# Sixteen products that nobody reads, between the last up products of each layer and the loop for further experts

## The chip, the core and the metric

The kernel runs on one core of one Trainium2 chip. The metric is the device time of one execution in microseconds (us). The engines are named as in the profile: PE is TensorE (PEld its weight loads), DVE is VectorE, ACT is ScalarE, POOL is GpSimd, and SP is SyncE, whose queue issues most of the transfers (DMAs). A name with a q (PEldq, SPq) is the sequencer of that engine, which takes its instructions in the order of the program.

## The reference

Two layers of a block with four mixers and a mixture of experts, on 256 tokens and 256 context tokens of width 1024. What matters here is the end of each layer: the experts, their sum, and what the next layer starts with.

```python
def moe(h, w_router, b_router, w1, w3, w2):
    ...
    gate = jnp.sum(jax.nn.one_hot(top_i, N_EXPERTS, dtype=F32) * top_w[..., None], axis=-2)
    out = 0.0
    for e in range(N_EXPERTS):
        he = jax.nn.silu(h @ w1[e]) * (h @ w3[e])
        out = out + gate[..., e:e + 1].astype(h.dtype) * (he @ w2[e])
    return out

def reference(...):
    for l in range(DEPTH):
        ...
        x = x + gt2 * moe(h2, router_w, router_b, moe_w1[l], moe_w3[l], moe_w2[l])
        ...
    return rms_norm(x, final_norm_g)
```

Each token goes to 2 of 16 experts. `h @ w1` and `h @ w3` are the up products, `he @ w2` the down products.

## The kernel before, in words

Each layer `l` runs through `mix` (input projection, the four mixers), `wout` and the router, and then `moe`. The tokens of an expert are gathered into a slot of fixed size (`SLOT`); the 16 slots run one after the other, as generators that `moe` advances in turn, so that the products of one expert lie between those of its neighbours. The weights of an expert are six blocks of 1 MB: 0 to 3 for the up products, 4 and 5 for the down products. SP fetches them ahead into rings of buffers (`fetch`, `pump`); the ring `raw` has three buffers, which experts, the input projection of the next layer (`in_win_dram`) and its modulation vectors (`in_wada_dram`) share.

The last expert of a layer, slot 15, has 64 rows (`expert32`). Its up products go to `sc`, two at a time in the two halves of the array: 32 products with 512 columns each. Then ACT copies `sc` to `al`, PE transposes `al` (`tp<-cst,al`), ACT and DVE make `silu(..) * ..` of it, and the 16 down products follow (`mm<-raw,ah`).

Between the up products and these transposes stands `extras(l)`: a loop over further slots of 128 rows, for experts with more tokens than their slot. How often it runs (`nx`, tile `rnx`) is known on the chip only; with these inputs it is 0 times in both layers, so that its body never runs. Every engine loads `rnx` into a register (line 2069), compares and branches (line 2070), and on the way past the loop all engines join: SP waits until each of its transfers has landed, each engine waits until its own work before the loop is done, and each reads the counts of all others before it goes on. These are the `EVENT_SEMAPHORE` instructions of line 2070.

Behind the loop come the down products, `combine_rows` (SP loads the sums of the other experts from the buffer `ybd` in HBM), and `combine`: for each piece of 128 rows by 512 columns PE adds the row of `ybd` (times the identity, `cst`) and the scattered result of the last expert in PSUM, and DVE, with POOL, adds it to the residual `yf`. Layer 0 has eight such pieces, layer 1 four. `self.gate_open += 1; self.pump()` lets SP go on to the weights of the next layer. After `combine` of layer 0 stands `ln1` of layer 1 with the input projection; after that of layer 1 `final`, the last norm and the store.

The order of the instructions within an engine is made by a scheduler from the priorities of the program; `tc.issue_after(x)` puts what stands under it directly behind instruction `x`. A helper records every operation, so that nearly all rows of the profile carry line 396.

Of the kernel before, what the change touches and what calls it, by code (L numbers as in the profile page):

```python
# [12 lines left out]
BF16 = mybir.dt.bfloat16  # L13
# [25 lines left out]
)  # L39
NRAW = 3  # L40
PARTED = (0, 4)
STAT = 2
RESERVE = (8, 8)
ADA_SLACK = (-1.0, 1.0)
# [16 lines left out]
TILE = [np.cumsum([0] + [-(-n // P) for n in SLOT[l]]).tolist() for l in range(L)]  # L61
ENDS = (STAT, NE - 1)

# [97 lines left out]
def _constants():  # L161
# [23 lines left out]
    for l in range(L):  # L185
        order = np.argsort([-n for n in SLOT[l][STAT:]], kind="stable")
        rk = np.full(16, -1)
        rk[STAT + order] = np.arange(NE - STAT)
        put(("rk", l), rk[None, :])
# [213 lines left out]
class Kern:  # L403
# [167 lines left out]
    def fetch(self, src):  # L571
        l = self.l
        n2, n3, n4 = BUFS[f"R{l}"]["raw2"], BUFS[self.scope]["raw3"], PARTED[l]
        r = self.wi % (n2 + NRAW + n3 + n4)
# [479 lines left out]
    def put(self, *ts):  # L1054
        for t in ts:
            (self.lent if id(t) in self.lentids else self.own).append(t)
# [671 lines left out]
    def route(self, l, NT):  # L1728
# [66 lines left out]

        nd = NE - STAT
        key, cap = f([P, 16], "key"), f([P, 16], "cap")
# [5 lines left out]
        along = lambda t: t[:, None, :].to_broadcast([P, nd, nd])  # L1803
        tt(big, along(key[:, STAT:]), down(key[:, STAT:]), op=ALU.is_gt)
        nc.vector.reduce_sum(rk, big, axis=AX.X)
        tt(sel, along(rk), down(self.C(("rk", l))[:, STAT:]), op=ALU.is_equal)
        nc.vector.memset(cap[:, 0:STAT], float(SLOT[l][0]))
# [141 lines left out]
    def moe(self, l, route):  # L1949
        nc, tc = self.nc, self.tc  # L1950
        self.yi, self.gi, self.wi = 0, 0, len(self.pre)
        xg, sl = {}, {}
        both = lambda e: [e] + ["x"] * (l == 0 and e == TWO)
        gens, srcs = {}, {}

        def source(e):
            if e not in srcs:
                srcs[e] = (self.wdyn(l, self.rt["idx"][0:1, e - STAT:e - STAT + 1]) if e >= STAT
                           else lambda c: self.I["wmoe"][self.wpos(l, e, c)])
            return srcs[e]  # L1960

        def begin(e):
            if self.whole(l, e):
                t = TILE[l][e]
                half = (self.row2[:, t:t + 1], self.slot_of(self.rt["tab2"][:, t])[1]) if SLOT[l][e] == HALF else None
                gens[e] = self.expert32(l, source(e), (xg.pop(e), *sl[e]), SLOT[l][e], half, last=e == NE - 1)
            else:
                gens[e] = self.expert(l, source(e), [(xg.pop(n), *sl[n]) for n in both(e)], min(P, SLOT[l][e]), ahead=NPRE * (e == 0))
            next(gens[e])

        first, i = self.first_slots(l)
        xg.update(enumerate(first))
        with tc.issue_after(i.ins):
            for _ in range(3):
                next(route)
        for e in range(NE):
            for n, t in zip(both(e), range(TILE[l][e], TILE[l][e + 1])):
                sl[n] = self.slot_of(self.rt["tab"][:, t])
        self.row2 = self.sx([P, TILE[l][NE]], "rrow2", I32)
        begin(0)  # L1980
        next(gens[0])
        for e in range(NE):
            if e == NE - 1:
                self.combine_g2(l)
                while self.wi < len(USE[l]):
                    self.pre.append(self.fetch(source(USE[l][self.wi][0])(USE[l][self.wi][1])))
            if STAT <= e + 2 < NE:
                for n in both(e + 2):
                    xg[n] = self.gather(l, *sl[n], m=min(P, SLOT[l][e + 2]))
            if e == 0:  # L1990
                nc.gpsimd.tensor_scalar(self.row2, self.rt["tab2"][:, :, 0], 2.0, self.half, op0=ALU.mult, op1=ALU.add)

            with tc.issue_after(self.rt["slots"].ins) if e == 0 else ExitStack():
                for j in range(2):
                    if e or j:
                        next(gens[e])
                    if e:
                        next(gens[e - 1], None)
                next(gens[e])
            if e:  # L2000
                next(gens[e - 1], None)
            if e + 1 in ENDS:
                for _ in gens[e]:
                    pass
                begin(e + 1)
                continue
            if e + 1 < NE:
                begin(e + 1)
            next(gens[e])


        self.extras(l)
        for _ in gens[NE - 1]:
            pass
        with tc.issue_after(self.last_y.ins):
            self.combine_rows(l)
        self.gate_open += 1
        self.pump()
        with tc.issue_after(self.last_y.ins), tc.issue_after(self.last_mm.ins):
            self.combine(l)  # L2020
# [399 lines left out]
```

## Time and profile before

| | |
|---|---|
| median of 3 runs | 1255.08 us (1253.22 to 1255.55) |
| the profiled execution | 1252.16 us, of which its span, first to last instruction, is 1250.5 us |
| busy: PE, DVE, ACT, POOL | 89%, 54%, 40%, 14% of the span |
| mean granted clock of PE | 0.946 of full speed |
| DMA, mean over the span | 267 GB/s |
| layer 0: last up product ends, transposes behind the loop start | 688.2 us, 695.0 us |
| layer 1: the same | 1221.2 us, 1224.8 us |

Times in the rows are microseconds from the start of the span. The granted clock 1.00 is 2.4 GHz, 0.50 is 1.2 GHz; a row of a stretch in which it changed shows a value between.

### The profile page before, as it was taken

Reading aid. Unit: us, or ns where it says so; the run is one execution under the profiler, and the core shown is the slowest. Engines: PE = TensorE matmul, PEld = TensorE weight load, DVE = VectorE, ACT = ScalarE, POOL = GpSimd, SP = SyncE. Lnnn points to the kernel's source line nnn. Section 1 sums busy time; section 2 is a strip of 40 time slices with the busy share of each in tenths; the row PEclk is TensorE's granted clock in tenths of the full one; section 3 lists DMA queues with packets and bytes.
Section 4 is the critical chain, followed back from the end, with each engine's and each line's share of the span. In section 5 each row is a group of like instructions: output and inputs, shape, how many; then the busy total and the mean of one; then the engine's idle time right before and its main releaser. Section 6 shows DMA issues by size and latency. Waiting matters only on the chain. (4 is left out here: it accounts for less than half of the span.)

```text
span 1250.5 us, 16252 instructions
## 1 busy us (share of the span) xinstructions
PE 1107.6 (89%) x5537; PEld 684.9 (55%) x5537; DVE 679.4 (54%) x1761; ACT 496.8 (40%) x818; POOL 169.5 (14%) x210
## 2 busy tenths in 40 slices
PE   4999999997995999999888779999986599999974
PEld 2677677765884766555444257776675233333321
DVE  6496579788668863554434548779897200000003
ACT  5231652667324853554434333283662121111112
POOL 0100200100003420211100000010010321111102
PEclk9999999998896999999989889999888699999997
DMA  8673654352936998999993735355358999999992
GB/s 307 246 275 110 221 214 160 136 181 93 366 139 228 353 353 309 359 373 378 383 381 124 299 147 198 101 205 192 129 180 341 381 373 390 371 398 387 397 408 101
DMA packets 66809, 334.08 MB, mean 267 GB/s; under 512 B 13389, under 2 KB 14893, under 8 KB 34977
## 3 DMA queue, kind: packets, MB, share of 16 engines
q1 hardware_dynamic: 54864, 312.39, 65.7%
q0 software_dynamic: 11424, 19.54, 6.0%
q8 instruction: 46, 0.75, 0.2%
q10 hardware_dynamic: 432, 1.05, 0.2%
q14 instruction: 43, 0.34, 0.1%
HBM read 317.54 MB, written 19.15 MB: 269 GB/s over the span
## 5 line engine op out<-in xcount | busy, mean ns | idle before, releaser
L396 DVE TENSOR_TENSOR lo<-raw,hi 128x1024 fp32r<-128x1024 f32 x172 | 206.1, 1221 | 122.0 <-ACT hi L396 120.8
L396 PE MATMUL sc<-raw,ah 128*64 128x512 f32 (+3 forms) x750 | 212.4, 602 | 6.4 <-DMA raw<-in_wmoe_dram 4.4
L396 ACT CAST hi<-raw 128x1024 fp32r<-128x1024 f32 x169 | 171.7, 1048 | 101.8 <-PE mm L396 53.4
L396 DVE TENSOR_TENSOR ah<-al,tp 128x256 f32<-128x256 f32 x21 | 8.8, 420 | 232.9 <-ACT al L396 232.9
L396 PEld LDWEIGHTS sc<-raw,ah 128*64 128x64 f32 (+3 forms) x750 | 62.9, 142 | 117.3 <-issue 100.2
L396 PE MATMUL mm<-hi,ah 128*128 128x512 f32 (+3 forms) x264 | 109.1, 417 | 6.0 <-ACT hi L396 5.6
L396 PE MATMUL mm<-raw,ah 128*64 128x512 f32 (+3 forms) x378 | 110.2, 620 | 3.5 <-DVE rel L396 1.9
L396 PE MATMUL mm<-lo,ah 128*128 128x512 f32 (+3 forms) x264 | 107.6, 407 | 1.6 <-DVE lo L396 1.5
L396 PE MATMUL mm<-hi,al 128*128 128x512 f32 (+3 forms) x264 | 106.9, 407 | 0.3 <-DVE al L396 0.3
L396 PE MATMUL mm<-ah,hi 128*128 128x512 f32 (+1 forms) x224 | 87.0, 393 | 0.8 <-DVE ah L396 0.8
L396 PE MATMUL mm<-ah,lo 128*128 128x512 f32 (+1 forms) x224 | 83.8, 375 | 0.9 <-DVE lo L396 0.9
L396 PE MATMUL mm<-al,hi 128*128 128x512 f32 (+1 forms) x224 | 83.7, 374 | 0.0
L396 PE MATMUL sc<-hi,ah 128*128 128x512 f32 (+3 forms) x176 | 73.6, 419 | 3.7 <-ACT hi L396 3.7
L396 PE MATMUL sc<-lo,ah 128*128 128x512 f32 (+3 forms) x176 | 72.2, 410 | 3.1 <-DVE lo L396 2.9
L396 PE MATMUL sc<-hi,al 128*128 128x512 f32 (+3 forms) x176 | 71.9, 408 | 1.8 <-DVE al L396 1.8
L396 PE MATMUL ad<-raw,cT 128*32 128x256 f32 (+1 forms) x512 | 68.2, 519 | 4.9 <-DMA raw<-in_wada_dram 3.4
L396 PEld LDWEIGHTS mm<-raw,ah 128*64 128x64 f32 (+3 forms) x378 | 33.9, 147 | 65.3 <-issue 55.3
L396 PEld LDWEIGHTS mm<-hi,ah 128*128 128x128 f32 (+3 forms) x264 | 49.7, 189 | 28.9 <-issue 7.8
L396 PEld LDWEIGHTS mm<-lo,ah 128*128 128x128 f32 (+3 forms) x264 | 50.0, 189 | 16.0 <-DVE lo L396 4.9
L396 PEld LDWEIGHTS mm<-hi,al 128*128 128x128 f32 (+3 forms) x264 | 49.9, 189 | 11.7 <-DVE al L396 1.0
L396 PEld LDWEIGHTS mm<-ah,hi 128*128 128x128 f32 x224 | 42.2, 191 | 23.0 <-issue 12.2
L396 POOL DMA_INDIRECT xg<-h2d,rtab x29 | 32.8, 1131 | 123.3 <-PE tp L396 115.1
(434 smaller groups left out, 1817.7 us busy)
## 6 DMA issues: line engine op xcount, KB each, us to landing
raw<-in_wmoe_dram SPq DMA_DIRECT2D x168, 1024.0 KB
raw<-in_wada_dram SPq DMA_DIRECT2D x32, 1024.0 KB
raw<-in_win_dram SPq DMA_DIRECT2D x24, 1024.0 KB
raw<-in_wmoe_dram SPq DMA_DIRECT2D x48, 512.0 KB
raw<-in_wad_dram SPq DMA_DIRECT2D x16, 1024.0 KB
raw<-in_wout_dram SPq DMA_DIRECT2D x8, 1024.0 KB
x<-in_tok_dram SPq DMA_DIRECT2D x8, 512.0 KB
raw<-ybd SPq DMA_DIRECT2D x6, 512.0 KB
```

The source lines that it names most:

```text
L396: r = f(*a, **k)
```

## The change

A new table `WARM` gives a count for each layer, and `moe` issues that many products directly behind the last up product of slot 15, ahead of `extras`: the constant `ones_b` (128 by 128, bf16, all ones) with the first 512 bf16 columns of the table of constants `cst`. All write the same PSUM buffer of the pool `mm`, each from the start, and nothing reads it.

```diff
+WARM = (16, 16)
...
+        ps = self.psmm()
+        with tc.issue_after(self.last_mm.ins):
+            for _ in range(WARM[l]):
+                nc.tensor.matmul(ps, lhsT=self.ones_b, rhs=self.cst.bitcast(BF16)[:, 0:512], start=True, stop=True)
         self.extras(l)
         for _ in gens[NE - 1]:
             pass
```

On PE, at the loop of layer 1, the last up products (`sc<-raw,ah`) stand before directly ahead of the load of `rnx`; the wait for PE_49, PE's own count, is the one for its work before the loop.

```order
L396 MATMUL sc_10216<-raw_10200,ah_10190 64x512
L396 MATMUL sc_10216<-raw_10204,ah_10190 64x512
L2069 TENSOR_LOAD rnx_8954 [waits DVE_49]
L2070 COMPARE_AND_BRANCH
L2070 UNCONDITIONAL_BRANCH [waits PE_49]
```

Now, in the same place, with 16 weight loads and 16 products:

```order
L397 MATMUL sc_10233<-raw_10217,ah_10207 64x512
L397 MATMUL sc_10233<-raw_10221,ah_10207 64x512
L397 LDWEIGHTS ones_b
L397 MATMUL mm_10251<-cst,ones_b 128x512 [waits PE_49]
L397 LDWEIGHTS ones_b
L397 MATMUL mm_10251<-cst,ones_b 128x512
...
L2074 TENSOR_LOAD rnx_8971 [waits DVE_49]
L2075 COMPARE_AND_BRANCH
L2075 UNCONDITIONAL_BRANCH [waits PE_49]
```

The new products stand between the last up products and the join, whose wait for PE's count now takes them in. The same 32 instructions stand ahead of the loop of layer 0.

On SP, ahead of the loop of layer 0, the last block of the last expert (`raw_6052`) is followed by the join, which waits for all transfers. Before:

```order
L396 DMA raw_6050<-in_wmoe_dram 128x2048 [waits DMAHW1_49,PE_49]
L396 ISA
L396 DMA raw_6052<-in_wmoe_dram 128x2048 [waits DMAHW2_49,DVE_49]
L2069 TENSOR_LOAD rnx_3739 [waits DVE_49]
L2070 COMPARE_AND_BRANCH
L2070 UNCONDITIONAL_BRANCH [waits SP_sequencer_49,DMAHW0_49,DMAHW1_49,DMAHW2_49,DMAHW3_49,DMAHW4_49,DMAHW5_49,DMAHW6_49,DMAHW7_49]
```

Now:

```order
L397 DMA raw_6052<-in_wmoe_dram 128x2048 [waits DMAHW2_49,DVE_49]
L2074 TENSOR_LOAD rnx_3739 [waits DVE_49]
L2074 ISA x2
L397 DMA raw_6359<-in_win_dram 128x2048 [waits DMAHW6_49,DVE_49]
L2075 COMPARE_AND_BRANCH
L2075 UNCONDITIONAL_BRANCH [waits SP_sequencer_49,DMAHW0_49,DMAHW1_49,DMAHW2_49,DMAHW3_49,DMAHW4_49,DMAHW5_49,DMAHW6_49,DMAHW7_49]
```

The first block of the next layer's input projection (1 MB) has moved from behind the loop to ahead of it.

On SP, directly behind the loop of layer 0, before:

```order
L2069 ISA x2
L396 DMA raw_6342<-in_win_dram 128x2048
L396 DMA raw_6344<-in_win_dram 128x2048
L396 DMA raw_6336<-ybd_222 128x1024 x2
L396 DMA raw_6339<-ybd_222 128x1024 x2
L396 DMA raw_6346<-in_wada_dram 128x2048 [waits PE_49]
```

Now:

```order
L397 DMA raw_6361<-in_win_dram 128x2048
L397 DMA raw_6363<-in_wada_dram 128x2048 [waits PE_49]
L397 DMA raw_6353<-ybd_222 128x1024 x2
L397 DMA raw_6356<-ybd_222 128x1024 x2
L397 DMA raw_6483<-in_wada_dram 128x2048 [waits DVE_49]
```

The first block of `in_wada_dram`, which waits for PE, has moved ahead of the four loads of `ybd`. With it one product of that block (`ad<-raw,cT`) has moved ahead of `combine` on PE, and the first two splits of the first `in_win_dram` block (`hi<-raw` on ACT, `lo<-raw,hi` on DVE) have moved ahead of the last expert's scaling. In layer 1 no instruction but the new ones has moved, and the rest of the program stands as before.

## Rows read from the trace of the kernel before

**Rows 1.** The page, its first line.

```profile
span 1250.5 us, 16252 instructions
```

**Rows 2.** Chain of work that ended last: start us, us, what.

```profile
1226.84 5.82 PE mm L396 x16
```

**Rows 3.** Timeline, end of layer 1: start us, us, engine, what, xcount [idle before <-releaser].

```profile
1217.59 3.65 PE L396 MATMUL sc<-raw,ah 128*64 128x512 f32 x14 [0.76 <-SPq L2070]
...
1224.78 1.12 PE L396 MATMUL tp<-cst,al 128*128 128x128 f32 x4 [3.55 <-SPq L2070]
1225.90 0.81 SPq L396 DMA_DIRECT2D raw<-ybd  x2
...
1229.71 4.67 POOL L396 TENSOR_TENSOR raw<-raw,raw 128x1024 f32<-128x1024 f32 x2 [17.33 <-DMA raw<-ybd]
```

**Rows 4.** Line 2070, layer 1, by stretches: xcount, ns min/median/max, first to last start us.

```profile
L2070 PEldq EVENT_SEMAPHORE  x13: 51/51/51, 1221.3 to 1224.4; - x13
...
L2070 PEldq EVENT_SEMAPHORE  x3: 51/51/51, 1221.8 to 1222.0; - x3
...
L2070 SPq EVENT_SEMAPHORE  x3: 17/17/17, 1224.0 to 1224.1; - x3
...
L2070 SPq EVENT_SEMAPHORE  x11: 27/28/28, 1224.8 to 1225.4; - x11
```

**Rows 5.** Stretches, layer 1: us, busy PE PEld DVE ACT POOL, PE clock, DMA share, GB/s.

```profile
1224.70:1226.00 1.30, 1.12 (x4) 0.72 (x4) 0.00 (x0) 0.07 (x1) 0.00 (x0) 0.50 0.01 6
...
1231.00:1232.00 1.00, 1.00 (x6) 0.31 (x4) 0.00 (x0) 0.00 (x0) 1.00 (x1) 0.90 0.00 0
```

**Rows 6.** Timeline of PE at full clock: single products, four transposes, 16 paired products.

```profile
663.33 0.39 PE L396 MATMUL sc<-hi,al 128*80 128x512 f32 x1
...
668.37 0.40 PE L396 MATMUL sc<-hi,ah 128*80 128x512 f32 x1
...
1149.47 0.66 PE L396 MATMUL tp<-cst,al 128*128 128x128 f32 x4 [0.68 <-ACT al L396]
...
1154.18 3.60 PE L396 MATMUL mm<-raw,ah 128*64 128x512 f32 x16
```

**Rows 7.** Timeline of PE, then a stretch as in rows 5.

```profile
672.20 0.49 PE L396 MATMUL tp<-cst,s 80*128 80x80 f32 x4 [0.78 <-DVE s L396]
...
674.00:678.00 4.00, 3.72 (x10) 2.04 (x10) 1.95 (x3) 0.59 (x2) 0.00 (x0) 0.60 0.02 6
```

**Rows 8.** Timeline, end of layer 0 and start of layer 1.

```profile
695.04 1.11 PE L396 MATMUL tp<-cst,al 128*128 128x128 f32 x4 [6.79 <-SPq L2070]
695.92 0.81 SPq L396 DMA_DIRECT2D raw<-in_win_dram  x2
696.77 2.15 SPq L396 DMA_DIRECT2D raw<-ybd  x4
697.08 6.14 PE L396 MATMUL mm<-raw,ah 128*64 128x512 f32 x16 [0.93 <-DVE rel L396]
703.27 7.86 SPq L396 DMA_DIRECT2D raw<-in_wada_dram  x3
704.67 1.13 PE L396 MATMUL mm<-raw,cst 128*128 128x512 f32 x2 [1.45 <-DMA raw<-ybd]
...
717.72 0.73 PE L396 MATMUL sc<-raw,ah 64*128 64x512 f32 x2
720.41 0.69 DVE L396 TENSOR_TENSOR yf<-yf,s 128x512 f32<-128x512 f32 x1
...
730.32 1.91 PE L396 MATMUL ad<-raw,cT 128*32 128x512 f32 x2 [2.83 <-DMA raw<-in_wada_dram]
```

**Rows 9.** Lines 2069 and 2070, layer 0, as in rows 4.

```profile
L2069 SPq TENSOR_LOAD <-rnx x1: 274/274/274, 686.2 to 686.2; - x1
...
L2070 SPq EVENT_SEMAPHORE  x8: 17/28/28, 694.3 to 695.0; - x8
```

**Rows 10.** A stretch of layer 0, as in rows 5.

```profile
690.00:691.00 1.00, 0.00 (x0) 0.00 (x0) 0.00 (x0) 0.00 (x0) 0.00 (x0) 1.00 0.97 385
```

## The prediction

> **What bounds the kernel now.** I read the page first: a span of 1250.5 us [rows 1], and PE busy for 89% of it. PE sets the pace, so the question is what PE does at the two places of the change. I then read the chain that ended last, which goes through the down products behind the loop of layer 1: 16 in 5.82 us [rows 2]. The timelines of the two loops came next, then the waits of line 2070, and last the granted clock in short stretches.
>
> At the loop of layer 1 the last up products run from 1217.59 for 3.65 us, so to 1221.24, and PE then stands for 3.55 us until the transposes at 1224.78 [rows 3]. Two things make up this pause. SP's counts for the landed transfers end at 1224.0 to 1224.1. PE's own sequencer sees its own work done at 1221.3, reads its first counts at 1221.8 and its last at 1224.4, and the transposes start 0.4 us later [rows 4]. Behind the pause the granted clock is 0.50, and it is on its way back only at about 1231 [rows 5]. The four transposes take 1.12 us there [rows 3] against 0.66 at full clock, and the 16 down products 5.82 us [rows 2] against 3.60 [rows 6]. That is 0.46 and 2.22 us, 2.7 us in all, which the slow clock costs in layer 1.
>
> At the loop of layer 0 the last up product ends at 688.2, and the transposes wait 6.79 us, until 695.04 [rows 8]. Here the transfers end last: SP reads its counts for them from 694.3 on [rows 9], and while PE stands still the transfers run at 385 GB/s, 97% busy [rows 10]. The transposes take 1.11 and the products 6.14 us, so this place pays for the slow clock too. Behind them the path is `ybd`: PE waits 1.45 us for its first rows and starts to combine at 704.67 [rows 8].
>
> **The change, part by part.** *The products themselves.* At full clock, single products of this width start 22 intervals apart between 663.33 and 668.37 [rows 6], 5.04 / 22 = 0.229 us each. Sixteen take 3.7 us. The weight loads beside them run on PEld; I count them at nothing, because the rows of that stretch have theirs inside the 0.229. Writing one PSUM buffer sixteen times could make them wait for each other; the rows do not show that pattern, and I bound it by the paired products, 3.60 / 16 = 0.225 us [rows 6], which would be no change, and by the slow ones, 5.82 / 16 = 0.364 us [rows 2], which would be 2.1 us more. I take 0.229.
>
> *Layer 1.* The products run from 1221.2 to about 1224.9, and the join waits for them. What PE needs from there is read from before: 0.5 us to the first count (1221.3 to 1221.8), twelve more counts at about 0.1 us each, and 0.4 us to the transposes [rows 4], together 2.1 us. In the pause of before, the early counts passed while SP was still waiting; now they all lie behind the products. The transposes start at 1224.9 + 2.1 = 1227.0 instead of 1224.78, **+2.2 us**. SP's transfers had landed at 1224.0, so they end last no more. The loads of `ybd` (issued 1225.90) and POOL's additions to them (1229.71, 4.67 us) [rows 3] are not behind PE, as SP reads its last counts at 1225.4 [rows 4], after 1224.9: they stay covered.
>
> What comes back depends on the clock. If the remaining pause of 2.1 us leaves it at 1.00, the 2.7 us return and the layer ends with 2.2 - 2.7 = -0.5. If it falls as before, but later, the transposes run at full clock and the products slow throughout: 16 products would take 2 x 3.60 = 7.2 us, 1.4 more than now, less 0.46 for the transposes, and the layer ends near 2.2 + 1.4 - 0.46 = +3.1; call it +2.9, as a slow stretch that began later may also end within them. A short pause of PE need not be safe: in another stretch the longest wait shown is 0.78 us, and the clock of the next microseconds, 674 to 678, is 0.60 although PE was busy for 3.72 of 4 us [rows 7]. So I take a value nearer the slow end, **+1.9**, and keep -0.5 and +2.9.
>
> The Trainium skill, "TensorE: Matmul & The Clock Gate", section "Why this matters for your kernels", says to leave no long idle gap between bursts of matmuls, since the clock falls back after one. Taken at its word, a pause shortened to some two microseconds would keep its clock, and the sum would have -0.5 in this place. By that rule the stretch of rows 7 should have kept its clock as well, and it did not, so this trace agrees only in part; I keep it as a rival.
>
> *Layer 0, the join.* PE's products end at 688.2 + 3.7 = 691.9, before SP's transfers: by themselves they cost nothing. The cover is the landing of the weights, until 694.3 [rows 9]. But the order moved a 1 MB block of `in_win_dram` ahead of the join, which waits for every transfer. At 385 GB/s [rows 10] 1 MB takes 1.05 / 0.385 = 2.7 us. With the queue already 97% busy it cannot hide; I take +2.5, from nothing (if its buffer came free late and the others had slack) to 2.9. The transposes start at about 697.5. PE's pause is then 697.5 - 691.9 = 5.6 us, hardly shorter than 6.79 [rows 8], so the clock will be down again, and the down products end at 706.0 instead of 703.2.
>
> *Layer 0, SP's queue.* Before, the four loads of `ybd` were issued at 696.77, and `in_wada_dram` behind them at 703.27, when the last down product (697.08 + 6.14 = 703.22) had released its buffer [rows 8]. Now the first wada block stands ahead of the `ybd` loads, and its wait for PE holds them. They are issued at about 706.4 instead of 696.8, some 9.6 us late, behind 1 MB on the same engines. From issue to use a `ybd` load took 3.8 us in layer 1 (1225.90 to 1229.71) [rows 3]. With 1.05 / 0.385 = 2.7 us for the block ahead, less 1 us for the overlap of issue and transfer, the first rows are there at about 706.4 + 3.8 + 1.7 = 711.9. PE's combining, which began at 704.67, begins **7.2 us** later. It took from 704.67 to 717.72 + 0.73 = 718.45, 13.8 us, so it ends at 725.7 (up to 3.4 more if the clock falls in the wait), and DVE's last `yf`, before at 720.41 + 0.69 = 721.10 [rows 8], ends at 727 to 730.5: +6 to +9.4, as two splits that DVE had in front of it are now done earlier.
>
> *Given back.* Before, PE stood 2.83 us for a wada block until 730.32 [rows 8]. A later combination uses this wait up; that block is later too, so I take 1 to 3 us. Layer 0 then costs **+6**, with ends at +3 (DVE +6, all of the wait used) and +9.4 (none of it).
>
> *The sum.* 1.9 + 6.0 = +7.9 us. The profiled execution took 1252.16 us, 2.92 below the median of the runs, 1255.08. On it the change gives 1260.1; on the median, **1263.0 us**.
>
> **The rivals.** *The clock stays up in layer 1 alone.* For it: the pause shrinks from 3.55 to 2.1 us. Against it: [rows 7]. Layer 1 gives -0.5, and with +6 the sum is +5.5, 1260.6 us: still slower. This is the time by the skill's rule.
>
> *The late `ybd` is absorbed.* If the wada block's wait ends earlier than the last down product, or the rows of `ybd` come faster than I think, DVE and the 2.83 us wait [rows 8] take up the rest: layer 0 near +0, layer 1 -0.5 to +1.9, in all 0 to +2, about 1256 us. Against it: before, wada was issued within 0.1 us of the end of the last down product.
>
> *Faster: the clock stays full behind both loops.* Decided by a granted clock of 1.00 at the transposes in both layers. Layer 1 then gains 0.5, and up to 2.1 if PE reads its counts beside the products, so that the transposes start 0.5 us behind them (1225.4, +0.6, less 2.7). In layer 0 transposes and products are (1.11 - 0.66) + (6.14 - 3.60) = 3.0 us shorter, the down products end at 703.0, as before, and wada is no longer late; what is left of the late `ybd` would have to vanish in the 2.83 us. The best case is -3.4, 1251.7 us. Against it: in layer 0 PE still pauses 5.6 us.
>
> **How the numbers follow.** The forecast, both costs with the slow clock, has 0.62; the clock in layer 1 alone 0.18; absorbed 0.13; faster 0.07. A measurement of this kernel tells a change of 0.2%, 2.5 us, from none. The first two cases lie above that, so slower has 0.80, the absorbed case gives same 0.13, and faster 0.07. The range goes from the lower bounds, layer 0 +3 and layer 1 -0.5, less 1 for part of the absorbed case (1256.5), to +12 of a possible 9.4 + 2.9 (1267.0).
>
> **What would show it.** Right: sixteen `mm<-cst,ones_b` for some 3.7 us behind each loop's up products; in layer 1 the transposes some 2.1 us behind the last of them, at a clock that falls soon after; in layer 0 the transposes near 697.5, a wada issue at 706 with the `ybd` issues right behind it, and a wait of PE for `ybd` of some 6 us. Wrong: a clock of 1.00 through the down products, `ybd` issued before the down products end, the products beside the join without delay in layer 1, or a start of the combination in layer 0 before 708.

## The result, and the profile after

| | before | changed |
|---|---|---|
| median of 18 runs each | 1255.38 us | 1262.81 us |
| lowest and highest | 1253.22, 1261.65 us | 1259.45, 1275.07 us |
| ratio, with 95% interval | | 1.0072 (1.0051 to 1.0092) |
| profiled execution, its span | 1252.16, 1250.5 us | 1262.72, 1261.1 us |

The change is slower by about 7.4 us between the medians; the forecast was 1263.0. The ratios here and below are not the quotients of the two medians, which would be 1.0059 here (that of the means is 1.0073). The runs of the changed kernel lie in two groups: 13 from 1259.45 to 1265.13, and five from 1272.15 to 1275.07. No run of before in this comparison is above 1261.65. The second group was not in the forecast, whose range ended at 1267.

The timeline at the end of layer 0 in the changed kernel (start us, us, engine, line, what, xcount, idle before and its releaser), which answers to [rows 8]:

```profile
682.14 7.09 PE L397 MATMUL sc<-raw,ah 128*64 128x512 f32 x32
689.16 3.63 PE L397 MATMUL mm<-cst,ones_b 128*128 128x512 bf16 x15
698.80 1.11 PE L397 MATMUL tp<-cst,al 128*128 128x128 f32 x4 [6.01 <-SPq L2075]
700.84 6.48 PE L397 MATMUL mm<-raw,ah 128*64 128x512 f32 x16 [0.93 <-DVE rel L397]
707.36 0.33 SPq L397 DMA_DIRECT2D raw<-in_wada_dram  x1
707.74 2.17 SPq L397 DMA_DIRECT2D raw<-ybd  x4
712.37 1.91 PE L397 MATMUL ad<-raw,cT 128*32 128x512 f32 x2 [5.05 <-DMA raw<-in_wada_dram]
714.22 2.08 PE L397 MATMUL mm<-raw,cst 128*128 128x512 f32 x2
...
729.96 0.69 DVE L397 TENSOR_TENSOR yf<-yf,s 128x512 f32<-128x512 f32 x1
730.68 1.12 SPq L397 DMA_DIRECT2D x1d<-yf  x2
731.91 0.90 SPq L397 DMA_DIRECT2D raw<-in_wada_dram  x1
...
740.39 1.91 PE L397 MATMUL ad<-raw,cT 128*32 128x512 f32 x2 [4.09 <-DMA raw<-in_wada_dram]
...
765.39 1.06 PE L397 MATMUL ad<-raw,cT 128*32 128x512 f32 x6
```

The first and the last row frame the layer-0 stretch that I use from here on: from the start of the last expert's up products to the six `ad` products in the next layer's mixers. It takes 765.39 - 682.14 = 83.25 us. The same two rows of before:

```profile
681.16 7.09 PE L396 MATMUL sc<-raw,ah 128*64 128x512 f32 x32
...
756.44 1.06 PE L396 MATMUL ad<-raw,cT 128*32 128x512 f32 x6
```

There it takes 75.28 us, so layer 0 costs 8.0 us in this pair of executions. The reader should see three things inside. The new products end at 692.8, but the transposes wait until 698.80 for SP. The loads of `ybd` are issued at 707.74, behind the wada block, which had waited for the down products. And PE pauses 5.05 us, does the wada block's product (x2 in the profile), and only then begins to combine. (Where a row of new products says x15 or x23, the profile lacks one record; 16 or 24 were issued.)

The end of layer 1, which answers to [rows 2, 3]:

```profile
1227.32 3.65 PE L397 MATMUL sc<-raw,ah 128*64 128x512 f32 x14 [0.78 <-DMA raw<-in_wmoe_dram]
...
1230.90 3.63 PE L397 MATMUL mm<-cst,ones_b 128*128 128x512 bf16 x15
...
1236.51 0.66 PE L397 MATMUL tp<-cst,al 128*128 128x128 f32 x4 [1.98 <-issue]
...
1238.09 5.35 PE L397 MATMUL mm<-raw,ah 128*64 128x512 f32 x16 [0.93 <-DVE rel L397]
```

From the end of the up products (1230.97) to the transposes it is 5.54 us, where it was 3.54 [rows 3]: +2.0. The transposes now run at full clock, the down products partly; how much of that is the products' doing is taken up at the end. Stretches of the same execution (us, busy PE, PEld, DVE, ACT, POOL, PE clock, DMA share, GB/s):

```profile
1236.50:1238.00 1.50, 0.66 (x4) 0.42 (x4) 0.39 (x2) 0.38 (x1) 0.00 (x0) 1.00 0.84 248
1238.00:1243.50 5.50, 5.41 (x17) 1.57 (x18) 0.60 (x5) 0.01 (x1) 4.35 (x2) 0.69 0.32 126
```

The spans differ by 10.6 us: 1.0 before the layer-0 stretch (682.14 against 681.16), 8.0 in it, 0.8 from there to the last up products of layer 1 (461.93 against 461.15 us), and 0.9 behind them (33.78 against 32.91). The 1.0 and the 0.8 lie where the change moves no instruction: executions differ by that much, and the first of these rows starts anywhere between 680.68 and 686.86 in the profiles of this study.

### The profile page after: what moved, and what is told of

Same layout as the page of the kernel before. It is cut to its first block, busy times and chain, and to the rows that moved or that the text cites. A ratio compares the mean times of both kernels' runs of the same rounds, so it can differ in the third digit from the quotient of the medians.

```text
span 1261.1 us, 16313 instructions
## 1 busy us (share of the span) xinstructions
PE 1115.4 (88%) x5567; PEld 687.9 (55%) x5569; DVE 677.7 (54%) x1761; ACT 497.0 (39%) x818; POOL 169.5 (13%) x210
## 5 line engine op out<-in xcount | busy, mean ns | idle before, releaser
L397 PEld LDWEIGHTS mm<-hi,ah 128*128 128x128 f32 (+3 forms) x264 | 49.8, 190 | 28.9 <-issue 7.8
L397 PE MATMUL tp<-cst,xg 64*128 64x64 f32 (+4 forms) x264 | 29.4, 250 | 22.8 <-DMA xg<-h2d,rsrc 16.5
```

Of the source, the lines that this page charges most:

```text
L397: r = f(*a, **k)
```

## The experiments

**Theory.** The products cost little; what they moved on SP in layer 0 costs most: a block ahead of the join, and `ybd` behind a wada block. **Rivals:** products cost their own duration wherever they stand (3.7 us a layer); or the clock decides.

### One layer at a time

```diff
-WARM = (16, 16)
+WARM = (0, 16)
```

> Sixteen products in layer 1 alone; the order of layer 0 is that of before. Theory (the moved transfers of layer 0 cost most; the products cost what they add on PE's way to the join): the products end about 3.7 us behind the up products, the transposes start about 2.0 us later than before, the transposes take 0.66 us and the down products some 5.4 us; in all +1 us, ratio 0.999 to 1.002. Rival (the products cost their own duration wherever they stand): +3.7 us, ratio 1.003.

Measured: 1257.38 us against 1255.31, ratio 1.0004 (0.9983 to 1.0024). The interval leaves out the +3.7 us of the rival (1.003). The timeline of PE at the loop of layer 1:

```profile
1226.70 3.63 PE L396 MATMUL mm<-cst,ones_b 128*128 128x512 bf16 x16
...
1232.42 0.66 PE L396 MATMUL tp<-cst,al 128*128 128x128 f32 x4 [2.10 <-issue]
1234.01 6.51 PE L396 MATMUL mm<-raw,ah 128*64 128x512 f32 x16 [0.93 <-DVE rel L396]
```

As expected up to the transposes; the down products took 6.51 us, where the changed kernel had 5.35.

```diff
-WARM = (16, 16)
+WARM = (16, 0)
```

> Sixteen products in layer 0 alone, with the order on SP that comes with them. Theory: all but 1 us of the change is here, +7 to +9 us, ratio 1.0055 to 1.0072. Rival (products cost their duration): +3.7 us, ratio 1.003.

Measured: 1261.97 us, ratio 1.007 (1.0037 to 1.0103): the cost is in layer 0, as the theory says. Four of the twelve runs took 1271.95 to 1276.24 us, and the profile is of such a one (1274.74). Its timeline, and below it the stretch of the combination (us, PE busy, PE clock, DMA share, GB/s):

```profile
715.14 1.91 PE L396 MATMUL ad<-raw,cT 128*32 128x512 f32 x2 [5.13 <-DMA raw<-in_wada_dram]
716.98 2.08 PE L396 MATMUL mm<-raw,cst 128*128 128x512 f32 x2
```

```profile
717.00:742.20 25.20, 25.20 (x33) 0.50 0.35 141
```

This is what makes the second group, as far as profiles show it. Behind the pause for wada and `ybd` PE combines at a granted clock of 0.50 (1.2 GHz) from first to last, 25.2 us, though it is busy all the time. Before, the same work stood behind a pause of 1.45 us [rows 8] and ran at 1.00; in the profiled execution of the changed kernel the clock came back after the first pieces:

```profile
704.60:718.50 13.90, 13.83 (x36) 1.00 0.83 329
```

```profile
714.20:729.20 15.00, 15.00 (x37) 0.91 0.59 239
```

The first is before, the second the changed kernel. So the combination costs 13.9, 15.0 or 25.2 us, by the clock alone.

### Products without the move, and the move without products

```diff
-    def pump(self):
+    def pump(self, behind=None):
...
+            if behind:
+                self.tc.add_manual_dep(i.ins, behind.ins.name, mybir.DependencyInfo(mybir.DependencyClass.Sync, mybir.DependencyReason.DATA), reason="behind the loop")
+                behind = None
...
-        self.pump()
+        self.pump(self.first_tp if l == 0 else None)
```

With `WARM = (16, 0)`. `first_tp` is the first transpose behind the loop.

> Sixteen products in layer 0, but the first in_win_dram block waits for the first transpose behind the loop, so that the order on SP is that of before. Theory: the products end before SP's transfers have landed, the transposes start when they did (some 7 us after the last up product), and the total is 0 +- 1 us, ratio 0.999 to 1.001. Rival (products cost their duration): +3.7 us, ratio 1.003. Second rival (the clock is kept by the shorter pause): -1 to -3 us.

Measured: 1256.33 us, ratio 1.0005 (0.9986 to 1.0023). Sixteen products in layer 0 cost nothing that can be measured; the rival's +3.7 us (1.003) lies outside the interval:

```profile
680.68 7.09 PE L396 MATMUL sc<-raw,ah 128*64 128x512 f32 x32
687.70 3.63 PE L396 MATMUL mm<-cst,ones_b 128*128 128x512 bf16 x16
694.95 1.12 PE L396 MATMUL tp<-cst,al 128*128 128x128 f32 x4 [3.62 <-SPq L2077]
...
704.26 1.12 PE L396 MATMUL mm<-raw,cst 128*128 128x512 f32 x2 [1.92 <-DMA raw<-ybd]
```

The layer-0 stretch is 755.08 - 680.68 = 74.40 us against 75.28. The pause is shorter by the products (3.62 against 6.79), and the transposes are as slow as before (1.12). The down products took 5.35 us instead of 6.14, but `ybd` landed no earlier: PE waited 1.92 us for it instead of 1.45. Nothing was lost and nothing won.

```diff
+        if l == 0:
+            self.gate_open += 1
+            self.pump(1)
         self.extras(l)
...
+        if l == 0:
+            self.pump()
-        with tc.issue_after(self.last_y.ins):
+        with tc.issue_after(self.last_y.ins), tc.issue_after(self.last_load.ins) if l == 0 else ExitStack():
             self.combine_rows(l)
...
```

No products; `pump(1)` issues one block, and `last_load` is the last load of `pump`, here the wada block.

> No products at all; in layer 0 the first in_win_dram block is issued ahead of the loop and the first in_wada_dram block ahead of the ybd loads, as in the changed kernel. Theory: the whole cost of layer 0 appears, the transposes some 2.7 us later, the combination starting about 9 us later, +7 to +9 us, ratio 1.0055 to 1.0072. Rival (products cost their duration): 0, ratio 1.000.

Measured: 1259.38 us, ratio 1.0022 (0.9999 to 1.0045). The median is +4 us, half of what I expected; the ratio of the theory (1.0055) lies outside the interval, and no cost at all just inside it.

The loads stand in the places of the changed kernel, but this kernel leaves out a part of the change that matters: the wait for PE. In the changed kernel the first wada block goes into the buffer that the last down product reads. Here it goes into that of the first `in_win_dram` block, and in the program it waits for DVE, which splits that block, and not for PE:

```profile
703.31 5.11 PE L396 MATMUL mm<-raw,ah 128*64 128x512 f32 x16 [0.93 <-DVE rel L396]
...
705.33 1.21 DVE L396 TENSOR_TENSOR lo<-raw,hi 128x1024 fp32r<-128x1024 f32 x1
...
706.57 0.33 SPq L396 DMA_DIRECT2D raw<-in_wada_dram  x1
```

The block is issued when the second split ends (706.54), 1.85 us before the down products do (708.42). In the changed kernel it was issued 0.04 us behind their end (707.32, 707.36). PE's pause is 3.16 us here instead of 5.05, and the combination starts 27.54 us behind the first up product instead of 32.08. So the smaller cost does not show that the products in front take part in it.

The profile is again of a long run (1273.19 us): the combination begins at 712.83 and runs at 0.51:

```profile
712.80:737.80 25.00, 24.97 (x32) 0.51 0.38 154
```

One of twelve runs was of that length here, four of twelve with the products. Why they are rarer stays open; the shorter pause is one difference.

### The two moves apart

```diff
-WARM = (16, 16)
+WARM = (13, 0)
```

By the order of the programs (only thirteen was run), twelve or thirteen products put the `in_win_dram` block ahead of the join and leave the wada block behind `ybd`; ten move nothing, fourteen move both.

> Thirteen products in layer 0, none in layer 1: with this count the first in_win_dram block stands ahead of the join, but the in_wada_dram block stays behind the ybd loads. Measure: from the start of the last expert's up products to the six ad products of layer 1's mixers, 75.3 us before, 83.3 us in the changed kernel. Theory (two terms: the block ahead of the join, and ybd behind wada): the transposes start 2.5 to 2.9 us later against the up products than before, PE waits for ybd no longer than before (under 2 us), the stretch is 77 to 78.5 us, ratio 1.001 to 1.0025, and no run lies more than 10 us above the median. Rival (the join alone makes the cost): 83 us.

```diff
+        if l == 0:
+            self.gate_open += 1
+            self.pump()
-        with tc.issue_after(self.last_y.ins):
+        with tc.issue_after(self.last_y.ins), tc.issue_after(self.last_load.ins) if l == 0 else ExitStack():
             self.combine_rows(l)
...
```

Here without products, and the first wada block waits for PE, as in the changed kernel.

> No products and the first in_win_dram block behind the loop as before; in layer 0 the first in_wada_dram block stands ahead of the ybd loads. Theory: the transposes start as before (6.8 us behind the up products), the ybd loads are issued when the down products end, PE pauses some 5 us before it combines, the clock falls in that pause, and the stretch from the up products to the six ad products is 80 to 82 us, with some runs 10 us longer, where the combination runs at half clock to its end. Ratio of the medians 1.003 to 1.006. Rival (the join alone makes the cost): 75.3 us, ratio 1.000.

The first measured 1257.23 us, ratio 1.0007 (0.9991 to 1.0022); stretch 758.78 - 682.41 = 76.37 us, +1.1, a little under what was expected. The runs do not tell it from before; the stretch does, as it is 74.40 to 75.56 us in five of the six profiled executions with the order of before (the sixth, a long one, comes further down). Its timeline:

```profile
682.41 7.09 PE L396 MATMUL sc<-raw,ah 128*64 128x512 f32 x32
...
699.10 1.12 PE L396 MATMUL tp<-cst,al 128*128 128x128 f32 x4 [6.68 <-SPq L2074]
701.14 6.45 PE L396 MATMUL mm<-raw,ah 128*64 128x512 f32 x16 [0.93 <-DVE rel L396]
707.51 1.12 PE L396 MATMUL mm<-raw,cst 128*128 128x512 f32 x2
```

The transposes start 2.8 us later than in the profile of before (16.69 against 13.88 us from the first up product; 13.5 to 14.4 in all executions with nothing moved ahead of the join or held up by products), but the combination only 1.6 us (25.10 against 23.51): `ybd` is there when the down products end, and PE's 1.45 us wait for it [rows 8] has gone.

The second measured 1259.37 us, ratio 1.0029 (1.0009 to 1.005); stretch 762.15 - 682.37 = 79.78 us, +4.5. The longest of its eleven runs is 1266.68, so the runs that are 10 us longer did not show here.

```profile
695.88 1.11 PE L396 MATMUL tp<-cst,al 128*128 128x128 f32 x4 [6.43 <-SPq L2078]
697.93 6.33 PE L396 MATMUL mm<-raw,ah 128*64 128x512 f32 x16 [0.93 <-DVE rel L396]
709.42 1.92 PE L396 MATMUL ad<-raw,cT 128*32 128x512 f32 x2 [5.16 <-DMA raw<-in_wada_dram]
711.26 2.08 PE L396 MATMUL mm<-raw,cst 128*128 128x512 f32 x2
```

The transposes come as before, the pause of 5.16 us is there. Of the two moves the one past `ybd` is the dear one. Alone, the join's shift is half absorbed by the wait for `ybd`. Behind a wada block that waits for PE that wait should be no cushion, so that the 2.8 us would count in full: 2.8 + 4.5 = 7.3 of the 8.0 us. That sum is argued from single executions; no kernel here has both moves, with the wait for PE, and no products.

### Is it the pause?

```diff
+        if l == 0:
+            ps = self.psmm()
+            with tc.issue_after(self.last_mm.ins):
+                for _ in range(16):
+                    nc.tensor.matmul(ps, lhsT=self.ones_b, rhs=self.cst.bitcast(BF16)[:, 0:512], start=True, stop=True)
         with tc.issue_after(self.last_y.ins):
             self.combine_rows(l)
```

With `WARM = (16, 0)`; the new lines stand behind the last down product.

> Sixteen products in layer 0 ahead of the loop with the order of the changed kernel, and sixteen more behind the last down product, where PE waits for wada and ybd. Theory (the pause of 5 us lets the clock fall, and in some runs it stays at 0.50 through the whole combination, which then takes 25 us instead of 14): the combination runs at 1.00 or nearly so, no run lies above 1268 us, the median is about 1260 us, and the longest run comes down from 1276 us. Rival (the longer runs have another cause): a third of the runs stays at 1272 to 1276 us. Second rival (products behind the down products delay the combination): the median rises by 2 us or more.

Measured: 1259.68 us, ratio 1.0029 (1.0015 to 1.0043); all eleven runs from 1257.17 to 1261.88. The long runs are gone, where they had been four of twelve in layer 0 alone and five of eighteen in the changed kernel:

```profile
705.18 3.63 PE L396 MATMUL mm<-cst,ones_b 128*128 128x512 bf16 x16
710.20 1.06 PE L396 MATMUL ad<-raw,cT 128*32 128x512 f32 x8 [1.39 <-DMA raw<-in_wada_dram]
711.56 1.10 PE L396 MATMUL mm<-raw,cst 128*128 128x512 f32 x2 [0.29 <-DMA raw<-ybd]
```

The wait is still there, filled with work that nobody reads, and the combination is at full clock (1.10 us for a pair, 1.13 in [rows 8]; 2.08 at half). The kernel with layer 0 alone ran on another chip, but the next kernel, on the same chip as this one, had runs of up to 1271.90 us.

The pause alone does not decide, though. In the fourteen profiled executions of this study PE stood ahead of the combination, or of the wada block's product in front of it, for 3.16 to 5.16 us in five, and for 2.06 us or less in nine. All nine combined at full clock. Of the five, three ran at half clock to the end (pauses of 5.13, 3.93 and 3.16 us), and two came back within the first pieces (5.16 and 5.05).

```diff
-WARM = (16, 16)
+WARM = (24, 0)
```

With the order of before, as in the kernel of products without the move. (The label speaks of 8; layer 1 has none.)

> Twenty-four products in layer 0 with the order of before on SP, none in layer 1. Theory: they end about 5.5 us behind the up products, PE's pause shrinks to about 2 us, the transposes run at full clock (0.66 us), the down products in 4 to 5.5 us instead of 6.1, and the stretch from the up products to the six ad products is 73.5 to 75.5 us against 75.3 before and 74.4 with sixteen; ratio 0.998 to 1.001. Rival (the clock is slow behind the join whatever stands before it): 76 us, as the transposes start 0.8 us later and nothing comes back.

> The kernel with twenty-four products in layer 0 and the order of before once more, for its profile: ten of its twelve runs lay at 1259 to 1272 us, but the profile was that of a run of 1255. Theory (the products end so late that the join waits for PE, and the clock that falls behind them stays down through the combination in most runs): a longer run shows a granted clock of 0.50 in layer 0's combination, which takes 18 to 25 us instead of 14. Rival (another place, layer 1 or the mixers): the combination takes 14 us in a run above 1260 as well.

Measured: 1263.68 us, ratio 1.0057 (1.0034 to 1.0079), a miss: I expected no change. Ten of the twelve runs lie from 1259.30 to 1271.90 us. The first profile is of a short run (1255.12 us), with a stretch of 74.41 us as expected; the second of a run of 1266.53 us, with 85.67. The two timelines, short run first:

```profile
697.65 0.66 PE L396 MATMUL tp<-cst,al 128*128 128x128 f32 x4 [2.14 <-issue]
699.23 5.30 PE L396 MATMUL mm<-raw,ah 128*64 128x512 f32 x16 [0.93 <-DVE rel L396]
706.59 1.12 PE L396 MATMUL mm<-raw,cst 128*128 128x512 f32 x2 [2.06 <-DMA raw<-ybd]
```

```profile
697.04 0.66 PE L396 MATMUL tp<-cst,al 128*128 128x128 f32 x4 [2.14 <-SPq L2077]
698.62 3.65 PE L396 MATMUL mm<-raw,ah 128*64 128x512 f32 x16 [0.93 <-DVE rel L396]
706.20 1.43 PE L396 MATMUL mm<-raw,cst 128*128 128x512 f32 x2 [3.93 <-DMA raw<-ybd]
```

In the longer run the clock held and the down products took 3.65 us. But `ybd` lands when it lands: the 1.65 us that PE won became pause, 3.93 us of it, and the combination ran at half clock to its end:

```profile
706.20:730.80 24.60, 24.60 (x35) 0.51 0.51 209
```

In the six profiled executions with the order of before the combination starts 23.45 to 23.83 us behind the first up product, with no products ahead of it, with sixteen or with twenty-four. A quicker step ahead of this fixed landing cost 11 us in this execution; that the other runs above 1259 us are of the same kind is inferred.

### Two attempts at something better

Sixteen products in layer 0 and eight in layer 1, with the order of before:

> The likeliest to be quicker than before: sixteen products in layer 0 with the order of before, eight in layer 1, which end about 1.8 us behind the up products, before SP's transfers have landed. Theory: layer 0's stretch from the up products to the six ad products is 74 to 75.5 us, in layer 1 the transposes start 3.5 to 4 us behind the up products as before, and the total is the same within what can be measured: ratio 0.998 to 1.001. Rival (the shorter pause brings the clock back for good): 0.9975 or less.

Measured: 1256.11 us, ratio 1.0003 (0.9982 to 1.0023), stretch 756.78 - 681.22 = 75.56 us; no gain.

Then, since `ybd` is what the combination of layer 0 waits for, its loads first:

```diff
         self.gate_open += 1
-        self.pump()
-        with tc.issue_after(self.last_y.ins), tc.issue_after(self.last_mm.ins):
+        with tc.issue_after(self.last_row.ins):
+            self.pump()
+        with tc.issue_after(self.last_y.ins), tc.issue_after(self.last_mm.ins), tc.issue_after(self.last_load.ins) if l == 0 else ExitStack():
             self.combine(l)
```

`last_row` is the last `ybd` load. Once without products, once with twenty-four in layer 0:

> No products; in layer 0 the four ybd loads stand ahead of all loads for the next layer. If the landing of ybd is what the combination of layer 0 waits for, it starts when the last down product's result is split, 22 to 22.6 us behind the start of the up products instead of 23.5, and never after a long pause. What may take it back: the second and third wada blocks now stand behind stores of the residual on SP. Theory: stretch to the six ad products 73.5 to 78 us (75.3 before), no run above 1265 us, ratio 0.998 to 1.003. Rival (ybd is not what is waited for): the combination starts at 23.5 us as before.

> The same order with twenty-four products in layer 0. With the order of before, ten of twelve runs of this count were 4 to 16 us longer than that kernel's quickest, and the one profiled had paused 3.93 us for ybd and then combined at 0.50. Theory (it is the pause for ybd that lets the clock fall): with ybd first the pause is under 1.5 us, the combination runs at 1.00 and takes 14 to 15 us in the profile, and no run lies above 1262 us; the median falls from 1263.7 to 1253 to 1258 us. Rival (the twenty-four products themselves make the long runs): the median stays above 1260 us.

Measured: 1254.62 us, ratio 0.9991 (0.9974 to 1.0008), and 1254.43 us, ratio 0.9995 (0.9978 to 1.0012). With twenty-four products the median falls from 1263.7 to 1254.4, and no run is above 1259.21. The same products, the same pause at the join (2.08 us), and no pause for `ybd`:

```profile
696.78 3.65 PE L396 MATMUL mm<-raw,ah 128*64 128x512 f32 x16 [0.93 <-DVE rel L396]
...
700.37 1.13 PE L396 MATMUL mm<-raw,cst 128*128 128x512 f32 x2
...
721.48 1.94 PE L396 MATMUL ad<-raw,cT 128*32 128x512 f32 x8 [5.39 <-DMA raw<-in_wada_dram]
```

The up products start at 680.75 there, so the combination begins after 19.62 us, 3.9 earlier than before. Some of it is given back to a wait for wada of 5.39 us, where it had been 2.83 [rows 8]: the first products of the next layer's input projection (`mm<-ah,hi`) start at 729.35, 48.6 us behind the first up product, where it had been 51.0 (732.16). That execution is the shortest of the twelve (1250.11 us). Without products the combination began after 22.13 us, as expected, and the input projection after 51.2, so that all of the gain is given back. Neither kernel can be told from before; both are clear of the changed kernel.

## Why the prediction was right, and where it was not

- **Products.** 3.63 us for sixteen, against 3.7. In layer 0 they cost nothing that can be measured by themselves, shown by the kernel without the move.
- **Layer 1, the join.** Transposes +2.0 us, against +2.2. Right.
- **Layer 1, the clock.** The transposes ran at full clock and the down products slower, as the forecast had it, but only in part: from the end of the up products to the end of the down products it is 12.5 us in the changed kernel and 13.8 with products in layer 1 alone, 11.4 before: +1.1 and +2.4 around the +1.9. But the 11.4 is near the slow end of what happens without products. In the eleven profiled executions without any in layer 1 it is 9.7 to 11.6 us, with 10.25 in the middle, and in six of them the transposes behind the loop took 0.66 us: the 2.7 us which the forecast let the slow clock cost are not paid in every execution. Two of the eleven, the move without products and the join alone:

```profile
1244.28 0.66 PE L396 MATMUL tp<-cst,al 128*128 128x128 f32 x4 [3.47 <-SPq L2081]
```

```profile
1226.12 1.11 PE L396 MATMUL tp<-cst,al 128*128 128x128 f32 x4 [3.39 <-SPq L2074]
```

At the end of the span little of all this can be told: from the last up product to the end it is 30.1 and 31.4 us with sixteen products, and 28.9 to 32.0, with 30.3 in the middle, in the eleven. The ratio of layer 1 alone, 1.0004, allows anything from -2.1 to +3.0 us.
- **Layer 0, the join.** Transposes +2.8 us, against +2.5 (from one profile to another it is 1.6 to 3.2). Right; and PE's clock was down behind it, as said.
- **SP's queue.** Wada at 707.36 and `ybd` at 707.74; with the 1.0 us by which this execution was late already, the forecast's 706.4 is 707.4. Right. The combination started 8.6 us later (32.08 against 23.51 us from the first up product), against 7.2. About half of the difference is that the first `ybd` load landed 5.8 us behind its issue, so at about 713.6, where the forecast's 711.9 is 712.9 in this execution. The other half is a term that was left out: the wada block's own product stands ahead of the combination on PE, 1.91 us at half clock, and ends at 714.28.
- **Given back, 1 to 3 us.** This step failed. PE's later wait for wada did not shrink, it grew from 2.83 to 4.09 us. I took its landing for nearly fixed. But that block stands on SP behind stores of the residual that wait for the combination (`x1d<-yf` at 730.68, the block at 731.91; before it was issued at 722.33): it moves with what I thought would move into it.
- **The combination's clock, "up to 3.4 more".** Mis-sized most of all, and no row was given for the 3.4. It cost 1.1 us in the profiled execution (15.0 against 13.9) and some 11 us in the executions profiled of the long kind. That the five runs of the changed kernel above 1272 are of that kind is inferred from the kernel with products in layer 0 alone, which has the same instructions there; no long run of the changed kernel itself was profiled.

Two figures do not come out of the prediction's own terms: the end of the down products at 706.0, where 703.2 + 2.5 gives 705.7, and the best case of the faster rival, -3.4, of which layer 1 gives 2.1 and nothing shown gives the rest. The forecast does not rest on the second, and on the first by 0.3 us.

So it was partly luck that the number came out within 0.2 us: layer 0 cost 8.0 in the profiled execution and not 6, what layer 1 cost the runs do not resolve, and the runs of the second group lie above the range. The mechanism and the sign are shown: the order on SP in layer 0, not the products.

The Trainium skill, "TensorE: Matmul & The Clock Gate", section "Why this matters for your kernels", had been weighed as a rival: by its rule against long idle gaps, taken at its word, a short pause would keep the clock. In layer 1 the pause fell to 1.98 us and the clock of the products behind was 0.69; with twenty-four products in layer 0 a pause of 2.14 us was followed by down products of 5.30 us in one execution and of 3.65 in another. The runs bear the rule out only in part: the pause got short, and the clock went either way.

## What to carry to other kernels

Before pricing an added instruction by its duration, look at what a scheduler moves because of it, and at what each moved load then waits for: two loads that changed their place on another queue cost all that could be measured, and thirteen products instead of sixteen would have moved only one of them. A load that waits for PE, put ahead of loads that PE waits for, turns a queue into a chain; and when PE comes out of a pause into a long piece of work, it can pay for the pause a second time, in the clock of the whole piece. Speeding up the step ahead of a fixed landing can make that worse; move the landing first.

## What the runs showed of the hardware

- A granted clock of 0.50 stayed for 25.2 us while PE was busy for all 25.2 of them, and the same products ran at 1.00 for 13.9 us where the clock was up when they began. The first was not expected: I had allowed for a fall that is made good within a few microseconds.
- The same pause (2.08 to 2.14 us, with twenty-four products ahead) was followed by the 16 down products at full clock in two executions (3.65 us) and at a mixed clock in one (5.30 us). Behind the loop of layer 1, without products, pauses of 2.72 to 3.55 us were followed by four transposes at full clock in six executions (0.66 us), at half in three (1.11 to 1.12), and at a mixed clock in two; 3.47 us had the first outcome and 3.39 us the second. What decides it, no run here shows.
